# Where two units' weight forms are made, and when modulation 5 is computed, in a one-core mixer and feed-forward block

## The chip, the cores and the metric

The kernel runs on one core of a Trainium2 chip. The metric is the device time of one execution, in microseconds (us). Five engines take part, each with its own stream of instructions that it works through in order: TensorE (matrix products; in the profile PE, its weight loads PEld), VectorE (DVE), ScalarE (ACT), GpSimd (POOL) and SyncE (SP, which here only issues transfers). GpSimd can issue transfers too.

## The reference

One layer of a transformer-like block on 1024 tokens of width 1024, all in float32:

```python
px = modulate(x, mx[0], mx[1]) @ w_in            # 1024 x 4864
mix_x = token_mixers(px, ...)                     # a two-way gated scan with 4 heads, a short convolution, a spatial gate
x_new = layer_norm(x * ALPHA + mx[2] * (mix_x @ w_out), ln1_g, ln1_b)
ffn_x = conv_ffn(modulate(x_new, mx[3], mx[4]), ffn_up, conv_w, conv_b, ffn_down)
x_new = layer_norm(x_new * ALPHA + mx[5] * ffn_x, ln2_g, ln2_b)
```

The six modulations `mx` are rows of `silu(c) @ ada_w + ada_b`. In `conv_ffn` the product with `ffn_up` (1024 x 5632) gives two halves a and g of 2816 columns each; a goes through a 3x3 convolution over a 16 x 64 grid and a GELU, is multiplied by g, and then by `ffn_down`.

## The kernel before

**Split products.** A float32 matrix is written as a high part (rounded to TensorE's fp32r format) and a low part (the remainder), and a product is three TensorE products: high x high, high x low, low x high. ScalarE makes the high part with a copy, VectorE or GpSimd the low part with a subtraction (`split`).

**Stages.** `startup` normalises and transposes x and makes the first projections. `mixers` runs the projections of w_in, head by head, between the steps of the scan: `z_head(h)` is three projections (`proj`), each of 48 TensorE products; `scan_levels` and `scan_states` are mostly VectorE and ScalarE work. `out_proj` multiplies by w_out, one tile t of 128 tokens after another, eight in all: 48 products a tile, then the sum with x (`ly`), the layer norm (`ln_rows`), and, for two tiles at a time, `modulate2`, which normalises again (`norm2`) and transposes for the feed-forward part. The mixers' outputs are split for tile t + 2 (tiles `mh`, `ml`) while tile t is worked on. `ffn_up` makes 22 units of 128 columns of a and g, and `ffn_down` the last product.

**Forms.** In `ffn_up` a unit's two 2 x 2 blocks of products are made by a Strassen-like scheme with seven products instead of eight. For them seven forms of the unit's weights are needed: four of the weights' quarters (a11, a12, a21, a22) or sums of them (S1 = a21 + a22, S2 = S1 - a11, a11 - a21, a12 - S2), each split into a high and a low part: 128 x 2 x 512 numbers, 512 KB. Product k of a unit is 12 TensorE products of 512 columns, in the order k = 1, 2, 6, 5, 7, 3, 4. From unit 3 on, ScalarE and GpSimd make the forms on the fly (`prepare`, five products ahead). Unit 0 is multiplied plainly. The forms of units 1 and 2 are made beforehand and parked in device memory: `park` gives a list of steps (load, sums, one step for each form), and `out_proj` runs one of them after the fourth and the eighth weight tile of each half. All of a step's arithmetic is on GpSimd, which also issues the stores. Forms 1 and 2 of unit 1 are not parked: `load_form` makes them in tile t = 6 of `out_proj`, ScalarE the high part, GpSimd the low part.

**Order.** Up to the end of `out_proj` a scheduler orders each engine's instructions from a model of their cost and from priorities (program order, with loads and their splits far ahead). In `ffn_up` everything stays in program order (`pinned`). Work that may be done at any time lies in the list `self.aside`, and `step(n)` takes n pieces from it; `proj` calls `step(2)`. In `mixers` it is empty until the modulations 2 to 4 are put into it, ahead of head 3.

**Tiles.** Tag S has 13 buffers of 4 KB a partition, which the mixers, w_out and `ffn_up` share; tag W has six, for weights and forms; tag R four, for raw loads. PSUM has two pairs of banks (`psA`) and four single banks (`psB`).

**Modulation 5.** Its eight columns (40 to 47) are made in `ffn_up`, two in each of the units 5, 7, 9 and 11, after product 6: `ada_col` is one VectorE reduction of 128 x 1024 (in the profile CUSTOM_DVE_ANT_0 on `ada`), a read of the accumulator and a small sum. Unit f's VectorE work in order: the sum a after product 5, two products h of the unit before, the sum r after product 7, the other half of a after product 3, and then the convolution, eight operations on a pair of banks. ScalarE copies r after product 5, and `centre` writes the convolution's middle tap into the pair of banks that product 3 goes on with.

Nearly all instructions are recorded under line 57, a helper; they are told apart by tiles.

Of the kernel before, what the change touches and what calls it, by code (L numbers as in the profile page):

```python
# [7 lines left out]
F32 = mybir.dt.float32  # L8
F32R = mybir.dt.float32r
# [7 lines left out]
P = 128  # L17
# [50 lines left out]
class Builder:  # L68
# [433 lines left out]
    def mixers(self, head, vt, gc):  # L502
        hd = [head] + [dict() for _ in range(H - 1)]
        O = [None] * H
        self.consts2()
        self.scan_prep(hd[0], 0)
        cx = self.ctx_prep()
        sc = [self.short_conv(0, gc)]
        self.scan_levels(hd[0])
        self.ctx_states(*cx)  # L510
        self.scan_prep(hd[1], 1, self.z_head(1))
        O[0] = self.scan_states(hd[0], 0, vt)
        self.scan_levels(hd[1])
        self.scan_prep(hd[2], 2, self.z_head(2))
        O[1] = self.scan_states(hd[1], 1, vt)
        self.scan_levels(hd[2])
        self.sc = self.S(nm="silc")
        self.nc.sync.dma_start(self.sc, self.silc[0:1].broadcast_to([P, D]))
        self.aside += self.more_mods(16, 24)
        vt = self.v_pair(1)  # L520
        self.scan_prep(hd[3], 3, self.z_head(3))
        O[2] = self.scan_states(hd[2], 2, vt)
        self.scan_levels(hd[3])
        self.aside += self.more_mods(24, 40)
        self.gate_head(O[0], 0)
        sc.append(self.short_conv(1))
        O[3] = self.scan_states(hd[3], 3, vt)
        self.aside = self.wout_load(range(5)) + self.aside
        for h in range(1, H - 1):
            self.gate_head(O[h], h)  # L530
        sg = self.spatial_gate()
        self.gate_head(O[H - 1], H - 1)
        self.step(99)
        self.mix = O + sc + sg
# [385 lines left out]
    def out_proj(self, op):  # L920
        nc, a = self.nc, self.a
        for part in self.wout_load(range(5, KT), op):
            part()
        lng, lnb = (self.row(n, op.tile([P, D], F32, name=n)) for n in ("ln1_g", "ln1_b"))
        order, wh, wl = self.order, self.wh, self.wl
        mhl = {}
        self.parked = {}
        parks = self.park(op, 1, (6, 5, 7, 3, 4)) + self.park(op, 2, (1, 2, 6, 5, 7, 3, 4))

        def split(t):  # L930
            mh, ml = self.S((KT, P), F32R, nm="mh"), self.S((KT, P), F32R, nm="ml")
            for kt in order:
                self.split(self.mix[kt][:, t * P:(t + 1) * P], mh[:, kt, :], ml[:, kt, :])
            mhl[t] = mh, ml

        split(0)
        split(1)
        ys = {}
        for t in range(NT):
            mh, ml = mhl.pop(t)  # L940
            banks = [self.bank("A") for _ in range(2)]
            for c in range(2):
                s = slice(c * 512, (c + 1) * 512)
                for kt in order:
                    self.mm3(banks[c], mh[:, kt, :], ml[:, kt, :], wh[kt][:, s], wl[kt][:, s], kt == order[0], kt == order[-1])
                    if c == 1:
                        self.step(1)
                    if parks and kt in (order[3], order[7]):
                        parks.pop(0)()
            y = ys[t] = self.S(nm="ly") if t % 3 == 2 or t == 7 else self.At(nm="ly")  # L950
            nc.sync.dma_start(y, a["x"][t * P:(t + 1) * P])
            if t + 2 < NT:
                split(t + 2)
            if t in (2, 4):
                self.aside += self.modulate2([ys[t - 2], ys[t - 1]], t - 2)
            if t == 6:
                self.first = [self.load_form(1, 0), self.load_form(1, 1)] + [self.load_unit(a["wup"][f], (KT, P)) for f in (0, FT)]
                self.raws = {}
            for c in range(2):
                s = slice(c * 512, (c + 1) * 512)  # L960
                nc.vector.scalar_tensor_tensor(out=y[:, s], in0=y[:, s], scalar=ALPHA, in1=banks[c], op0=ALU.mult, op1=ALU.add)
            if t == 7:
                self.norm2([ys[j] for j in (4, 5, 6)])
            self.ln_rows(y, lng, lnb)
            nc.sync.dma_start(self.xnew[t], y)
        return [ys[t] for t in range(4, 8)]
# [36 lines left out]

    FORM = {1: "11", 2: "21", 3: "22", 4: "T4", 5: "T1", 6: "T2", 7: "T3"}

    def load_form(self, u, i):

        w = self.Wt((2, 512), nm="wf")
        with self.tc.high_priority(self.AHEAD):
            raw = self.Rt((4, P))  # L1010
            self.nc.sync.dma_start(raw, self.a["wup"][u][:, 4 * i:4 * i + 4])
            self.split(raw.rearrange("p k f -> p (k f)"), w[:, 0], w[:, 1], self.nc.gpsimd)
        return w

    def load_raws(self, u):
        ra, rg = self.S((2, 512), nm="raw"), self.S((2, 512), nm="raw")
        for r, f in ((ra, u), (rg, FT + u)):
            self.nc.sync.dma_start(r.rearrange("p j (k f) -> p (j k) f", f=P), self.a["wup"][f])
        self.raws[u] = dict(a=ra, g=rg)

    def park(self, op, u, ks):

        nc, pool = self.nc, self.nc.gpsimd
        r = {}

        def raws():
            for i, f in enumerate((u, FT + u)):
                r[i] = op.tile([P, 2, 512], F32, tag="raw", bufs=2, name=self.name("raw"))
                nc.sync.dma_start(r[i].rearrange("p j (k f) -> p (j k) f", f=P), self.a["wup"][f])

        def parts():
            return r[0][:, 0], r[0][:, 1], r[1][:, 0], r[1][:, 1]

        def sums():
            a11, a12, a21, a22 = parts()
            s = self.Wt((2, 512), F32, nm="ws")
            r["S1"], r["S2"] = s[:, 0], s[:, 1]
            pool.tensor_tensor(out=r["S1"], in0=a21, in1=a22, op=ALU.add)
            pool.tensor_tensor(out=r["S2"], in0=r["S1"], in1=a11, op=ALU.subtract)

        def sums2():
            a11, a12, a21, a22 = parts()
            pool.tensor_tensor(out=a12, in0=a12, in1=r["S2"], op=ALU.subtract)
            pool.tensor_tensor(out=a21, in0=a11, in1=a21, op=ALU.subtract)

        def one(k):
            a11, a12, a21, a22 = parts()
            src = {1: a11, 2: a12, 3: a12, 4: a22, 5: r.get("S1"), 6: r.get("S2"), 7: a21}[k]
            w = self.Wt((2, 512), nm="wp")
            pool.tensor_copy(w[:, 0], src)  # L1050
            pool.tensor_tensor(out=w[:, 1], in0=src, in1=w[:, 0].bitcast(F32), op=ALU.subtract)
            d = self.parked[u, k] = self.dp.tile([P, 2, 512], F32, name=self.name("wd"))
            nc.gpsimd.dma_start(d, w.bitcast(F32))
        one_ = lambda k: lambda: one(k)
        early = [k for k in ks if k < 3]
        return [raws, sums] + [one_(k) for k in early] + [sums2] + [one_(k) for k in ks if k not in early]

    def prepare(self, n):

# [6 lines left out]
        while self.prepared < min(n + 1, len(self.plan)):  # L1066
            u, k = self.plan[self.prepared]
            self.prepared += 1
            if (u, k) in self.parked:
                self.forms[u, k] = self.Wt((2, 512), nm="wf")  # L1070
                nc.sync.dma_start(self.forms[u, k].bitcast(F32), self.parked[u, k])
                continue
            r = self.raws[u]
            a11, a12, a21, a22 = r["a"][:, 0], r["a"][:, 1], r["g"][:, 0], r["g"][:, 1]
# [38 lines left out]
    def ffn_up(self, ys):  # L1113
# [45 lines left out]
        def sums(j):  # L1159
            b12, b22, b11 = v[j][:, 0], v[j][:, 1], xa[j]  # L1160
            return [lambda: tt(out=b22, in0=b22, in1=b12, op=ALU.subtract),
                    lambda: tt(out=b12, in0=b12, in1=b11, op=ALU.subtract),
                    lambda: tt(out=b11, in0=b22, in1=b11, op=ALU.add)]
# [109 lines left out]
        for f in range(3, FT):  # L1273
            if f + 2 < FT:
                self.load_raws(f + 2)
            if f in (5, 7, 9, 11):
                silc = self.S(nm="silc5")
                nc.sync.dma_start(silc, self.silc[0:1].broadcast_to([P, D]))
                ada = [self.S(nm="ada") for _ in range(2)]
                for i in range(2):  # L1280
                    nc.sync.dma_start(ada[i], self.a["ada"][35 + f + i])
            if f == last:
                ahead = self.down_first()
            while self.at < len(self.plan) and self.plan[self.at][0] == f:
                k = self.plan[self.at][1]
                step()
                if f == last:
                    ahead(k)
                if k == 6 and f in (5, 7, 9, 11):
                    for i in range(2):  # L1290
                        j = 35 + f + i
                        self.ada_col(j, silc, self.mods[:, j:j + 1], [ada[i]])
            if f == 12:
                self.gate5 = self.gate_line(5)
        self.prev.gelu()
# [276 lines left out]
```

## Time and profile before

| | |
|---|---|
| median of three runs | 1369.55 us (1369.33 to 1370.62) |
| the profiled execution | 1371.46 us, its span 1369.7 us |
| TensorE busy | 1284.1 us, 94% of the span |
| VectorE busy | 977.1 us, 71% |
| ScalarE busy | 528.3 us, 39% |
| GpSimd busy | 334.1 us, 24% |
| mean granted TensorE clock | 0.983 |
| moved by the transfer engines | 177.09 MB, mean 129 GB/s |

The span runs from the first to the last instruction of the program. By the time at which their tiles appear, the mixers run up to about 540 us, w_out from 540.9 to 661 us, `ffn_up` from there to about 1110 us, and `ffn_down` after that. The page's slices are 34.2 us long each, and a digit is the busy share in tenths. A row of the timeline gives start, length, engine, line, operation, the tiles written and read, and in brackets how long the engine stood idle before it and what released it. In a row of the windows each engine has its busy time and its count of instructions, and the last three numbers are the granted clock, the mean busy share of the 16 transfer engines and GB/s.

### The profile page before, as it was taken

Reading aid. Unit: us, or ns where it says so; the run is one execution under the profiler, and the core shown is the slowest. Engines: PE = TensorE matmul, PEld = TensorE weight load, DVE = VectorE, ACT = ScalarE, POOL = GpSimd, SP = SyncE. Lnnn points to the kernel's source line nnn. Section 1 sums busy time; section 2 is a strip of 40 time slices with the busy share of each in tenths; the row PEclk is TensorE's granted clock in tenths of the full one; section 3 lists DMA queues with packets and bytes.
Section 4 is the critical chain, followed back from the end, with each engine's and each line's share of the span. In section 5 each row is a group of like instructions: output and inputs, shape, how many; then the busy total and the mean of one; then the engine's idle time right before and its main releaser. Section 6 shows DMA issues by size and latency. Waiting matters only on the chain. (4 is left out here: it accounts for less than half of the span.)

```text
span 1369.7 us, 17583 instructions
## 1 busy us (share of the span) xinstructions
PE 1284.1 (94%) x6480; PEld 1074.6 (78%) x6480; DVE 977.1 (71%) x1712; ACT 528.3 (39%) x966; POOL 334.1 (24%) x279
## 2 busy tenths in 40 slices
PE   4999999999999999949998999999999999999997
PEld 3878988898888797737876877778888887887885
DVE  7868963778669587788797767776776664349447
ACT  4745443432432331135463434344444434323420
POOL 0000000000000000560027766677777740000000
PEclk9999999999999999969999999999999999999999
DMA  9662320023121353545452332332122218447532
GB/s 331 241 223 86 108 92 33 31 80 106 47 92 62 105 161 108 197 168 177 150 190 87 138 132 71 122 138 74 65 93 93 77 69 296 167 152 247 178 97 86
DMA packets 70406, 177.09 MB, mean 129 GB/s; under 512 B 8224, under 2 KB 10928, under 8 KB 70320
## 3 DMA queue, kind: packets, MB, share of 16 engines
q1 hardware_dynamic: 68304, 168.63, 36.2%
q0 software_dynamic: 2016, 7.34, 1.3%
q8 instruction: 51, 0.84, 0.2%
q14 instruction: 35, 0.29, 0.1%
HBM read 147.61 MB, written 28.33 MB: 128 GB/s over the span
## 5 line engine op out<-in xcount | busy, mean ns | idle before, releaser
L57 DVE SCALAR_TENSOR_TENSOR psA<-a,par,psA 128x945 f32<-128x945 f32 (+2 forms) x176 | 215.9, 1227 | 21.6 <-ACT psA L57 16.2
L57 PE MATMUL psA<-x,wf 128*128 128x512 f32 x708 | 175.7, 398 | 15.2 <-ACT psA L57 11.8
L57 PE MATMUL psB<-xk,wf 128*128 128x512 f32 x672 | 176.8, 390 | 1.0 <-ACT s L57 1.0
L57 PEld LDWEIGHTS psA<-x,wf 128*128 128x128 f32 x708 | 135.5, 192 | 46.6 <-ACT psA L57 14.3
L57 PEld LDWEIGHTS psB<-xk,wf 128*128 128x128 f32 x672 | 126.2, 188 | 27.9 <-ACT s L57 1.4
L57 POOL TENSOR_TENSOR wf<-raw,wf 128x512 fp32r<-128x512 f32 x95 | 124.5, 1322 | 62.8 <-ACT wf L57 62.7
L57 PE MATMUL psA<-xh,wh 128*128 128x512 f32 x320 | 127.4, 398 | 2.1 <-ACT wh L57 1.2
L57 PE MATMUL psA<-xh,wl 128*128 128x512 f32 x320 | 126.6, 396 | 0.1
L57 PE MATMUL psA<-xl,wh 128*128 128x512 f32 x320 | 126.6, 396 | 0.0
L57 POOL TENSOR_TENSOR ws<-raw 128x512 f32<-128x512 f32 x2 | 2.6, 1282 | 460.3 <-DMA raw<-in_wup 460.3
L57 DVE TENSOR_TENSOR dwl<-r,dwh 128x512 fp32r<-128x512 f32 x74 | 48.4, 688 | 81.1 <-ACT dwh L57 81.0
L57 PE MATMUL psB<-x,wf 128*128 128x512 f32 x384 | 104.7, 389 | 0.0
L57 PE MATMUL psB<-dwh,dh 128*128 128x512 f32 x296 | 98.5, 394 | 2.9 <-ACT dh L57 2.9
L57 PE MATMUL psA<-dwh,dh 128*128 128x512 f32 x296 | 97.3, 390 | 0.7 <-DVE fy L57 0.7
L57 PEld LDWEIGHTS psB<-x,wf 128*128 128x128 f32 x384 | 72.1, 188 | 15.4 <-issue 0.2
L57 ACT CAST dwh<-r 128x512 fp32r<-128x512 f32 x74 | 43.0, 619 | 102.8 <-PE psA L57 67.0
L57 ACT CAST wh<-r 128x512 fp32r<-128x512 f32 x76 | 44.6, 618 | 92.1 <-PE psA L57 64.5
L57 DVE TENSOR_TENSOR a<-psA,s 128x512 f32<-128x512 f32 x39 | 26.9, 691 | 72.1 <-PE psA L57 72.1
L57 DVE TENSOR_TENSOR wl<-r,wh 128x512 fp32r<-128x512 f32 x76 | 49.9, 685 | 36.1 <-ACT wh L57 22.8
L57 ACT CAST wf<-raw 128x512 fp32r<-128x512 f32 x95 | 58.5, 616 | 42.3 <-PE psA L57 27.4
L57 PEld LDWEIGHTS psA<-xh,wh 128*128 128x128 f32 x320 | 60.5, 189 | 14.2 <-ACT wh L57 1.6
L57 PEld LDWEIGHTS psA<-xh,wl 128*128 128x128 f32 x320 | 60.6, 189 | 12.5 <-DVE wl L57 0.5
(328 smaller groups left out, 2813.8 us busy)
## 6 DMA issues: line engine op xcount, KB each, us to landing
raw<-in_wup SPq DMA_DIRECT2D x42, 512.0 KB, 4.8
r<-in_w_down SPq DMA_DIRECT2D x82, 256.0 KB, 3.3
ada<-in_ada SPq DMA_DIRECT2D x32, 512.0 KB, 3.8
r<-in_win SPq DMA_DIRECT2D x56, 256.0 KB, 2.7
hr<-hd SPq DMA_DIRECT2D x41, 256.0 KB, 4.2
hd<-h SPq DMA_DIRECT2D x20, 512.0 KB, 3.0
adat<-in_ada SPq DMA_DIRECT2D x16, 512.0 KB, 6.9
wd<-wp POOLq DMA_DIRECT2D x12, 512.0 KB, 3.8
```

Source lines behind the costliest of these rows:

```text
L57: ins = f(*args, **kw)
```

## The change

1. `park` no longer works form by form on GpSimd. A unit is now done in four chunks, the k-th 128 columns of each quarter in one tile of 128 x 8 x 128: four quarters from device memory and the four sums S1, S2, a11 - a21 and a12 - S2, which VectorE makes (`sums(c)`, four operations of 128 x 128). `store(c)` then makes the high part of all eight with one ScalarE copy of 128 x 1024 and the low part with one VectorE subtraction; GpSimd only issues the two stores.
2. Unit 1's eight steps go into `self.aside` of `mixers`, behind `ctx_states`, so that the `step(2)` calls of the next projections take them; its tiles have tag S. Unit 2's eight steps run in `out_proj`, one after the products of each tile t.
3. A form is read back with two transfers, one for the high and one for the low part, in pieces of 128 numbers (`parked_form`). Forms 1 and 2 of unit 1 are read back in the same way at t = 6; `load_form` goes.
4. Modulation 5 is made one column in each of the units 4 to 11, after product 7 instead of 6, with the bias given to the reduction as its start value, so that the small sum goes.

```diff
         self.ctx_states(*cx)
+        self.parked = {}
+        self.aside += self.park(1, lambda dt: self.S((8, P), dt, nm="pk"))
         self.scan_prep(hd[1], 1, self.z_head(1))
...
-        parks = self.park(op, 1, (6, 5, 7, 3, 4)) + self.park(op, 2, (1, 2, 6, 5, 7, 3, 4))
+        parks = self.park(2, lambda dt: op.tile([P, 8, P], dt, tag="pk", bufs=2, name=self.name("pk")))
...
-                    if parks and kt in (order[3], order[7]):
-                        parks.pop(0)()
+            parks.pop(0)()
...
-                self.first = [self.load_form(1, 0), self.load_form(1, 1)] + [...]
+                self.first = [self.parked_form(1, 1), self.parked_form(1, 2)] + [...]
...
+        def sums(c):
+            r = t[c] = new(F32)
+            for i, f in enumerate((u, FT + u)):
+                nc.sync.dma_start(r[:, 2 * i:2 * i + 2], self.a["wup"][f].rearrange("p (j k) f -> p j k f", j=2)[:, :, c])
+            a11, a12, a21, a22, s1, s2, s3, s4 = (r[:, i] for i in range(8))
+            tt(out=s1, in0=a21, in1=a22, op=ALU.add)
+            tt(out=s3, in0=a11, in1=a21, op=ALU.subtract)
+            tt(out=s2, in0=s1, in1=a11, op=ALU.subtract)
+            tt(out=s4, in0=a12, in1=s2, op=ALU.subtract)
+        def store(c):
+            r, h = t[c], new(F32R)
+            nc.scalar.copy(h, r)
+            nc.gpsimd.dma_start(d[:, 0, c], h.bitcast(F32))
+            tt(out=r.bitcast(F32R), in0=r, in1=h.bitcast(F32), op=ALU.subtract)
+            nc.gpsimd.dma_start(d[:, 1, c], r)
+        return [lambda c=c, f=f: f(c) for c in range(4) for f in (sums, store)]
+
+    def parked_form(self, u, k):
+        w = self.Wt((2, 512), nm="wf")
+        i = {1: 0, 2: 1, 3: 7, 4: 3, 5: 4, 6: 5, 7: 6}[k]
+        for j in range(2):
+            self.nc.sync.dma_start(w[:, j].bitcast(F32).rearrange("p (c f) -> p c f", c=4), self.parked[u][:, j, :, i])
+        return w
...
-            if f in (5, 7, 9, 11):
-                silc = self.S(nm="silc5")
+            if 4 <= f < 12:
+                silc, ada = self.S(nm="silc5"), self.S(nm="ada")
                 nc.sync.dma_start(silc, self.silc[0:1].broadcast_to([P, D]))
-                ada = [self.S(nm="ada") for _ in range(2)]
-                for i in range(2):
-                    nc.sync.dma_start(ada[i], self.a["ada"][35 + f + i])
+                nc.sync.dma_start(ada, self.a["ada"][36 + f])
...
-                if k == 6 and f in (5, 7, 9, 11):
-                    for i in range(2):
-                        j = 35 + f + i
-                        self.ada_col(j, silc, self.mods[:, j:j + 1], [ada[i]])
+                if k == 7 and 4 <= f < 12:
+                    j = 36 + f
+                    nc.vector.tensor_tensor_reduce(out=ada, in0=ada, in1=silc, scale=1.0, scalar=self.par[:, C_ADAB + j:C_ADAB + j + 1],
+                                                   op0=ALU.mult, op1=ALU.add, accum_out=self.mods[:, j:j + 1])
```

More of the change, by code (lines that the diff above doesn't have):

```diff
@@ L926, in out_proj @@
         mhl = {}
-        self.parked = {}
-        parks = self.park(op, 1, (6, 5, 7, 3, 4)) + self.park(op, 2, (1, 2, 6, 5, 7, 3, 4))
+        parks = self.park(2, lambda dt: op.tile([P, 8, P], dt, tag="pk", bufs=2, name=self.name("pk")))
         def split(t):
@@ L956, in out_proj @@
             if t == 6:
-                self.first = [self.load_form(1, 0), self.load_form(1, 1)] + [self.load_unit(a["wup"][f], (KT, P)) for f in (0, FT)]
+                self.first = [self.parked_form(1, 1), self.parked_form(1, 2)] + [self.load_unit(a["wup"][f], (KT, P)) for f in (0, FT)]
                 self.raws = {}
@@ L1004 @@
     FORM = {1: "11", 2: "21", 3: "22", 4: "T4", 5: "T1", 6: "T2", 7: "T3"}
[L1006 to L1013, printed above, removed]
     def load_raws(self, u):
@@ L1019, in load_raws @@
         self.raws[u] = dict(a=ra, g=rg)
[L1021 to L1026, printed above, removed]
-            for i, f in enumerate((u, FT + u)):
[L1028 to L1056, printed above, removed]
@@ new lines, in park @@
+    def park(self, u, new):
+        nc, tt = self.nc, self.nc.vector.tensor_tensor
+        d = self.parked[u] = self.dp.tile([P, 2, 4, 8, P], F32, name=self.name("wd"))
+        t = {}
+        def sums(c):
+            r = t[c] = new(F32)
+            for i, f in enumerate((u, FT + u)):
+                nc.sync.dma_start(r[:, 2 * i:2 * i + 2], self.a["wup"][f].rearrange("p (j k) f -> p j k f", j=2)[:, :, c])
[11 more added lines that the diff above has]
+        return [lambda c=c, f=f: f(c) for c in range(4) for f in (sums, store)]
@@ L1068, in prepare @@
             self.prepared += 1
-            if (u, k) in self.parked:
-                self.forms[u, k] = self.Wt((2, 512), nm="wf")
-                nc.sync.dma_start(self.forms[u, k].bitcast(F32), self.parked[u, k])
+            if u in self.parked:
+                self.forms[u, k] = self.parked_form(u, k)
                 continue
```

## The prediction

> **What bounds the kernel now.** I read the page's slices first, then TensorE's waits, then the windows around each dip, and last the instructions there in order of time.
>
> ```profile
> span 1369.7 us, 17583 instructions
> PE   4999999999999999949998999999999999999997
> PEclk9999999999999999969999999999999999999999
> ```
>
> TensorE is busy nearly everywhere, so only its holes can be won. Slice 17 (from 582 us) is half empty, and the granted clock falls to 0.6 there. That is w_out, where GpSimd makes the parked forms. In these windows the pairs are PE, PEld, DVE, ACT and POOL busy time, then the granted clock:
>
> ```profile
> 540.90:585.90 45.00, 41.49 (x171) 31.61 (x171) 37.59 (x81) 13.63 (x50) 18.74 (x21) 1.00 0.47 172
> 585.90:600.30 14.40, 0.00 (x0) 0.00 (x0) 14.40 (x16) 1.25 (x2) 14.36 (x18) 0.58 0.26 106
> 600.30:612.10 11.80, 8.79 (x25) 6.47 (x26) 8.66 (x18) 5.23 (x12) 5.97 (x7) 0.50 0.70 272
> 612.10:648.00 35.90, 35.90 (x166) 28.50 (x165) 28.38 (x87) 18.05 (x56) 0.29 (x1) 1.00 0.47 159
> ```
>
> TensorE stands still for 14.4 us while VectorE and GpSimd are both full; then it works at half clock; after GpSimd falls silent it is full. The timeline says why (start, length, instruction, in brackets the idle time before it and its releaser):
>
> ```profile
> 568.07 0.73 PE L57 MATMUL psA<-wok,mh 128*128 128x512 f32 x2 [1.51 <-DVE ly L57]
> 600.35 0.48 PE L57 MATMUL psB<-ident,ly 128*128 128x128 f32 x1 [14.52 <-ACT ly L57]
> 607.20 0.90 PE L57 MATMUL psB<-ident,ly 128*128 128x128 f32 x3 [2.96 <-ACT ly L57]
> ...
> 599.05 1.24 ACT L57 ACTIVATE ly<-ly,nmt,rst 128x1024 f32<-128x1024 f32 x1 [15.10 <-DVE nmt L57]
> ...
> 549.19 0.28 DVE L57 TENSOR_TENSOR ml<-O,mh 128x128 fp32r<-128x128 f32 x1
> 589.64 5.47 DVE L57 TENSOR_TENSOR ml<-sgo,mh 128x128 fp32r<-128x128 f32 x2
> 595.03 3.14 DVE L57 TENSOR_TENSOR ml<-O,mh 128x128 fp32r<-128x128 f32 x1
> ...
> 595.55 2.47 POOL L57 TENSOR_TENSOR wp<-ws,wp 128x512 fp32r<-128x512 f32 x2
> ```
>
> A subtraction ml of 0.28 us takes 3.14 us and ends (598.17) just after two of GpSimd's (598.02). VectorE, in order, then reaches nmt late, ScalarE's ly waits 15.10 us for it, and the first transpose of modulate2 waits 14.52 us for ly. So VectorE's two-input operations wait for GpSimd's.
>
> The second loss is in ffn_up. The chain of waits shows the units' boundaries (12 products of 512 take 2.72 us, a unit of seven takes 19.04):
>
> ```profile
> 773.94 5.44 PE psB L57 x24
> ...
> 797.04 5.46 PE psB L57 x24
> ...
> 816.11 5.44 PE psB L57 x24
> ...
> 920.28 4.76 PE psB L57 x21
> ```
>
> Unit 5, with two ada columns, takes 23.10 us; unit 6, without, 19.07. From 773.94 to 920.28 there are seven units, 5 to 11: 146.34 us, 13.1 more than 7 x 19.04, all in the four units that carry columns.
>
> **The change part by part.** *GpSimd's forms leave w_out.* This takes away the hole (14.4), in the next 11.8 us everything but what 15 products of 512 (0.23 each, 2.72/12) and 10 transposes (about 0.13) cost at full clock, 4.8, so 7.0, and the 1.51 at 568: 22.9 us. It takes VectorE's waits too:
>
> ```profile
> L57 DVE TENSOR_TENSOR ml<-O,mh 128x128 fp32r<-128x128 f32 x32 | 17.5, 563 | 8.7 <-PE psA L57 5.4 <-PE psB L57 2.9 <-ACT mh L57 0.2
> L57 DVE TENSOR_TENSOR ml<-sgo,mh 128x128 fp32r<-128x128 f32 x16 | 10.0, 661 | 0.0
> L57 DVE TENSOR_TENSOR ml<-sco,mh 128x128 fp32r<-128x128 f32 x16 | 6.9, 467 | 0.0
> ...
> L57 DVE TENSOR_TENSOR kq<-kq,F 128x1024 f32<-128x1024 f32 x56 | 67.4, 1214 | 0.2
> ```
>
> The 64 ml subtractions took 34.4 us where 64 x 0.28 is 17.9: 16.5 us of waiting.
>
> *Unit 2's forms come to VectorE and ScalarE there.* A chunk costs VectorE four small operations (0.28) and one of 1024 (1.21, the kq row): 2.3 us, four chunks 9.3; ScalarE one copy of 1024, about 1.1 (twice the 0.61 of a 512 cast, below), 4.6 in all, where it is two thirds idle. VectorE's four windows above hold 89.0 us; less 16.5, plus 9.3, that is 81.8, against 107.1 - 22.9 = 84.2 us that TensorE would then need. VectorE is thus close behind TensorE. The copy and the differences queue ahead of split(t+2) and the ly sums, on which the transposes wait. What stays of stalls is between 0 (81.8 fits) and the whole 9.3; I take 3, since ml is not the only operation that got stretched, so that the true load is lower, but the load is uneven. Later, load_form's two casts and two GpSimd operations also go.
>
> *Unit 1's forms go among the mixers*: 9.3 us of VectorE, 4.6 of ScalarE, eight steps, six in z_head(1), two in z_head(2).
>
> ```profile
> 200.00:220.00 20.00, 20.00 (x90) 16.56 (x89) 3.98 (x6) 8.45 (x14) 0.00 (x0) 1.00 0.16 53
> ```
>
> In z_head(1) VectorE is busy 4 of 20 us and GpSimd not at all, so I count 0. The cover is TensorE's own full row; were it gone, the price is 9.3. New waits: each chunk's two loads stand on SP among the w_in loads and need one of 13 S tiles; behind a stuck load wait the next w_in pieces, behind a stuck difference on VectorE the wl splits. Those run about one projection ahead. Bounds -1 to +5 (half of the 9.3; a rearranged order can also gain).
>
> *Stores and loads.* GpSimd issues 16 stores instead of 12, at a time when it does nothing else. SP issues 16 chunk loads of 128 KB instead of four raws of 512 KB (half of them now among the mixers), and 28 form loads instead of 14 (12 wf, load_form's two), in 512-byte pieces instead of 4 KB; at 0.3 to 0.5 us an issue this fills no queue. At the start of ffn_up a form is eaten every 2.72 us:
>
> ```profile
> 698.00:702.00 4.00, 4.00 (x18) 2.96 (x17) 4.00 (x7) 3.90 (x8) 0.10 (x1) 1.00 0.98 388
> ...
> 636.00:637.00 1.00, 1.00 (x8) 0.86 (x8) 0.40 (x2) 1.00 (x4) 0.00 (x0) 1.00 1.02 401
> ```
>
> The forms now move at 388 GB/s with the transfer engines full; a microsecond of xr stores (1 KB pieces) shows 401. At 300 GB/s a form of 512 KB would take 1.7 us, under 2.72. No row has 512-byte pieces in bulk; I take 0, bounds 0 to +8. The Trainium skill ("DMA: Bandwidth & Descriptors", Specifications) puts the smallest transfer for line rate at 512 B; by it these loads would cost nothing more, and no row here shows it.
>
> *Modulation 5, one column a unit, after product 7.* SP loads silc eight times instead of four, a unit ahead of its use; two S tiles a unit are held instead of three every second one. The reduction, without the small sum behind it, moves from between the convolution and the sum a to behind the sum r. A unit without columns, and the old reductions of unit 7:
>
> ```profile
> 798.69 10.06 DVE L57 SCALAR_TENSOR_TENSOR psA<-a,par,psA 128x945 f32<-128x945 f32 x8 [0.85 <-ACT psA L57]
> 813.50 0.69 DVE L57 TENSOR_TENSOR r<-psB,r 128x512 f32<-128x512 f32 x1 [0.83 <-ACT wf L57]
> 816.22 0.69 DVE L57 TENSOR_TENSOR a<-psA,s 128x512 f32<-128x512 f32 x1 [2.03 <-PE psA L57]
> 827.73 2.27 DVE L57 CUSTOM_DVE_ANT_0 ada<-ada,silc 128x1024 f32<-128x1024 f32 x1
> 831.10 1.21 DVE L57 CUSTOM_DVE_ANT_0 ada<-ada,silc 128x1024 f32<-128x1024 f32 x1
> ...
> 809.76 0.61 ACT L57 CAST wf<-raw 128x512 fp32r<-128x512 f32 x1
> 811.50 0.59 ACT L57 COPY r<-psA 128x512 f32<-128x512 f32 x1 [1.13 <-DVE a L57]
> 812.12 0.78 ACT L57 ACTIVATE psA<-a,par 128x512 f32<-128x512 f32 x1
> ...
> 813.23 2.88 PE L57 MATMUL psA<-x,wf 128*128 128x512 f32 x12
> ...
> 813.52 1.29 POOL L57 TENSOR_TENSOR wf<-s,wf 128x512 fp32r<-128x512 f32 x1 [1.78 <-ACT wf L57]
> ...
> 817.26 1.31 POOL L57 TENSOR_TENSOR raw<-raw,s 128x512 f32<-128x512 f32 x1
> ```
>
> Between r's end (814.19) and the next a (816.22) VectorE waits 2.03 us: room for 1.21. If the reduction ends later by D, a and the convolution shift by D; ScalarE has 1.1 us of slack before r's copy and 0.3 before product 3, so TensorE pays only what D has over 1.4. GpSimd works from 813.52 to 818.57 (four operations, first and last shown), so the reduction may be held up. One operation long (it starts at 814.77) it ends at 816.0 and costs nothing; two long, at 817.2, D = 1.0, still nothing; three long, at 818.5, D = 2.3, it costs 0.9 a unit. I take 0 and the full 13.1; bounds 0 to 15. The Trainium skill ("SBUF — State Buffer", Who interferes with whom) says that a VectorE instruction with two SBUF inputs contends with a GpSimd one that reads SBUF, and that whichever issues first blocks the other until it is done; by that the reduction waits for one operation and the sum is mine. The 3.14 us row outlasted two, so the row leaves the rival below open.
>
> **The sum.** The profiled execution took 1371.46 us (span 1369.7). 1371.5 - 22.9 + 3 - 13.1 = 1338.5. It stands 1.9 above the median of the runs, 1369.55, so 1336.6, said as 1337.
>
> **The rivals.** A: VectorE becomes the bound of w_out and all 9.3 us come on the path instead of 3: 1343. For it speaks 81.8 of 84.2; against it that TensorE stayed full in 612 to 648 with VectorE at 28 of 36. B: the reduction waits for three GpSimd operations: 8 x 0.9, and a slow restart as in unit 5 (4.06 us lost for a wait of 2.2) about doubles it, 7 to 15 us: 1344 to 1352. For it: 813.52 to 818.57 has no gap. Against: the old ones lost 1.06 us at most. C: the mixers pay up to 5 for unit 1's steps: 1337 to 1342. D, the other side: the form loads of 512-byte pieces fall behind. Ten forms are eaten in a row after 700 us. To eat all 33 us each must come 3.3 late, one per 6.0 us, that is 87 GB/s; below this the kernel is slower than before (at 60 GB/s, 8.7 us a form, by 27: 1397). Against it stand 388 and 401 GB/s. E: the change does not do what it says, that is, the hole is VectorE's own load and stays: then only the 13.1 come, 1356. Against: the 0.28 against 3.14 us.
>
> **How the numbers follow.** My forecast (1330 to 1340) 0.55; A 0.14; B 0.13; C 0.08; D and all that turns the sign 0.04; E 0.06. The range 1327 to 1351 holds the forecast, A, C and most of B, some 0.87 at most by these chances. Two runs of this kernel tell apart about 0.2%, 2.7 us. Faster: 0.95; same 0.01; slower 0.04.
>
> **What would show it.** After: no slice under 8 between 540 and 680 us, granted clock 1.00 there, no GpSimd operation in w_out but stores, ml at 0.28 us; seven units 5 to 11 in 133 to 134 us, with ada reductions of 1.2 to 3.5 us behind r; the same full TensorE row in z_head(1) and (2); no wait of TensorE for a transfer of wf. It is wrong if a transpose in w_out still waits for ly over 5 us, if product 3 waits for ScalarE's psA in units 4 to 11, or if TensorE has new holes between 190 and 300 us.

## The result, and the profile after

| | before | after |
|---|---|---|
| median of the four runs | 1369.53 us | 1335.52 us (without the fourth 1335.19) |
| the profiled execution | 1371.46 us, its span 1369.7 | 1334.04 us, its span 1332.1 |
| TensorE busy | 1284.1 us, 94% | 1275.0 us, 96% |
| VectorE busy | 977.1 us | 963.9 us |
| ScalarE busy | 528.3 us | 536.7 us |
| GpSimd busy | 334.1 us | 307.0 us |

The ratio is 0.9746, 95% interval 0.9727 to 0.9766; the forecast was 1337, from 1327 to 1351. Three of the four times of after lie between 1334.04 and 1335.85 us; the fourth, 3283.34 us, is explained by nothing on record, and the ratio leaves it out. In a later series the same kernel took 1335.78 us (1334.16 to 1337.52).

The slices of after come first (33.3 us each). Slice 17 is full now, and the granted clock has no dip there:

```profile
span 1332.1 us, 17666 instructions
PE   4999999999999999999988999999999999999997
PEclk9999999999999999999998999999999999999999
```

The new dip, slices 20 and 21, is the beginning of ffn_up from 666 us; its losses were there before, 23 us later. A ledger by stage, from TensorE's first products of each stage in both traces, in us:

| stage | before | after | difference |
|---|---|---|---|
| start to the first product of w_out | 540.90 | 539.93 | -1.0 |
| w_out, to the first product of ffn_up | 120.08 | 97.07 | -23.0 |
| ffn_up to the end of unit 4 | 112.96 | 114.54 | +1.6 |
| units 5 to 11 | 146.34 | 133.51 | -12.8 |
| unit 12 to the first steady piece of w_down | 218.15 | 216.20 | -1.95 |
| the rest | 231.27 | 230.85 | -0.4 |

The two stages that were to gain bring 35.8 of the 37.6 us between the two spans. First w_out. Its windows after (PE, PEld, DVE, ACT, POOL busy time with counts, granted clock, share of the transfer engines, GB/s), and beside them z_head(1), which was shown before:

```profile
539.93:584.93 45.00, 44.26 (x187) 34.20 (x187) 40.16 (x122) 18.56 (x56) 2.13 (x4) 1.00 0.38 131
584.93:637.00 52.07, 50.45 (x230) 40.26 (x231) 44.26 (x127) 25.95 (x73) 2.13 (x4) 1.00 0.58 197
...
200.00:220.00 20.00, 20.00 (x90) 16.57 (x89) 6.68 (x12) 9.38 (x15) 1.83 (x4) 1.00 0.47 167
```

TensorE works 94.7 of 97.07 us at full clock. VectorE is busy 84.4 us in the stage. The same stage of before, as one window, shows what it was busy with:

```profile
540.90:660.98 120.08, 99.16 (x417) 77.01 (x417) 101.90 (x228) 41.33 (x125) 41.61 (x46) 0.90 0.46 165
```

VectorE had 20 instructions fewer there and was busy 101.9 us. The 20 are unit 2's (tiles pk). Without them the stage of after is busy 77.4 us: they last 9.0 us by themselves, but neighbouring records overlap by up to 0.1 us, so they add only 7.0. The instructions that both kernels have thus took 101.9 us before and 77.4 after, about 24 us of mere waiting. The groups name it: 17.9 us are ml (34.4 before; 8.5 + 4.0 + 4.0 = 16.5 after, 0.28 us each on average), 4.9 two operations on one column (nwt), 1.4 an operation of the layer norm (`ly`). The groups of after, with the new operations on pk of both units, at the prices taken for them:

```profile
L57 DVE TENSOR_TENSOR pk<-pk,pk 128x1024 fp32r<-128x1024 f32 x8 | 9.7, 1215 | 4.7 <-ACT pk L57 4.6
L57 DVE TENSOR_TENSOR ml<-O,mh 128x128 fp32r<-128x128 f32 x32 | 8.5, 283 | 0.2 <-PE psA L57 0.2
L57 ACT CAST pk<-pk 128x1024 fp32r<-128x1024 f32 x8 | 8.4, 1049 | 10.9 <-DVE pk L57 9.1 <-issue 1.9
L57 DVE TENSOR_TENSOR pk<-pk 128x128 f32<-128x128 f32 x32 | 8.2, 280 | 4.6 <-DMA pk<-in_wup 4.4
L57 DVE TENSOR_TENSOR ml<-sgo,mh 128x128 fp32r<-128x128 f32 x16 | 4.0, 284 | 0.0
L57 DVE TENSOR_TENSOR ml<-sco,mh 128x128 fp32r<-128x128 f32 x16 | 4.0, 284 | 0.0
```

Even an operation on one column had been held up (it has two inputs, vet and rst). The larger of the two groups on nwt, in the stage of before, and then in after:

```profile
L57 DVE TENSOR_TENSOR nwt<-vet,rst 128x1 f32<-128x1 f32 x12 | 5.3, 442 | 0.0
```

```profile
L57 DVE TENSOR_TENSOR nwt<-vet,rst 128x1 f32<-128x1 f32 x12 | 1.8, 149 | 0.0
```

TensorE's waits of after, from 540 to 1100 us (in total, times, longest): ly has 1.7 us left of 17.5, and the waits for psA 3.1 of 11.8.

```profile
PE psA L57 <- ACT h L57: 3.4, 1, 3.4
PE psA L57 <- ACT psA L57: 3.1, 2, 1.8
PE psB L57 <- ACT dh L57: 2.6, 1, 2.6
PE psB L57 <- ACT ly L57: 1.7, 2, 1.4
```

Then the units. In the chain of waits of after units 5 to 11, each of which has a column now, take 133.51 us, 19.07 each, the time of unit 6 without columns in before (unit 8, whose reduction lasted 2.19 us, took 19.27, the others 19.04):

```profile
751.54 5.44 PE psB L57 x24
770.58 5.44 PE psB L57 x24
789.62 5.44 PE psB L57 x24
...
866.01 5.44 PE psB L57 x24
885.05 5.44 PE psB L57 x24
```

The timeline of one unit shows how the reduction meets GpSimd (start, length):

```profile
787.00 0.69 DVE L57 TENSOR_TENSOR r<-psB,r 128x512 f32<-128x512 f32 x1 [0.82 <-ACT wf L57]
787.60 1.81 DVE L57 CUSTOM_DVE_ANT_0 ada<-ada,silc,par 128x1024 f32<-128x1024 f32 x1
789.73 0.69 DVE L57 TENSOR_TENSOR a<-psA,s 128x512 f32<-128x512 f32 x1 [0.31 <-PE psA L57]
...
787.04 1.29 POOL L57 TENSOR_TENSOR wf<-s,wf 128x512 fp32r<-128x512 f32 x1 [1.75 <-ACT wf L57]
788.30 2.27 POOL L57 TENSOR_TENSOR raw<-raw,raw 128x512 f32<-128x512 f32 x1
```

The reduction, 1.21 us long by itself, starts at 787.60 and ends 0.6 us later than it would alone: it waits for the one GpSimd operation under way (to 788.33). Then GpSimd's next operation lasts 2.27 instead of 1.29: now GpSimd waits. The sum a still finds 0.31 us of idle time ahead of it, so TensorE pays nothing.

### The profile page after: what moved, and what is told of

Read it like the earlier page. It is cut to its first block, busy times and chain, and to the rows that moved or that the text cites. A ratio compares the mean times of both kernels' runs of the same rounds, so it can differ in the third digit from the quotient of the medians.

```text
span 1332.1 us, 17666 instructions
## 1 busy us (share of the span) xinstructions
PE 1275.0 (96%) x6480; PEld 1069.2 (80%) x6480; DVE 963.9 (72%) x1744; ACT 536.7 (40%) x972; POOL 307.0 (23%) x249
## 5 line engine op out<-in xcount | busy, mean ns | idle before, releaser
L57 POOL DMA_DIRECT2D wd<-pk x16 | 8.7, 543 | 498.9 <-ACT pk L57 461.3
L57 PEld LDWEIGHTS psA<-xl,wh 128*128 128x128 f32 x320 | 60.2, 188 | 11.8 <-issue 0.2
```

The costliest lines, as they stand in the source:

```text
L57: ins = f(*args, **kw)
```

## The experiments

There are ten runs, in three series, each beside the kernel before on the same chip.

**The parts by themselves.** `mod5_only` is the kernel before with the new modulation 5; `forms_only` is the changed kernel with the old one.

> The kernel before with the new modulation 5 alone (one column in each of units 4 to 11, after product 7); the forms are made by GpSimd in w_out as before. Theory (the two gains are separate stretches of TensorE's path and add up): units 5 to 11 take 133.3 to 133.6 us instead of 146.3, the hole in w_out stays as it was, time 1356 to 1357. Rival (the change's halves need each other, or the gain in the units is given back at the start of w_down): 1360 to 1369.

> The changed kernel with the old modulation 5 (two columns in units 5, 7, 9 and 11, after product 6). Theory: w_out stays about 97 us long (540 to 637), units 5 to 11 take 146 us again, time 1347 to 1350, that is 13 more than the changed kernel; with the run of modulation 5 alone the two gains add up to the whole of 34 within 2. Rival (part of the w_out gain was only that units meet another phase of the clock): 1340 to 1346 or over 1351.

Measured: modulation 5 alone 1356.43 us against 1368.40, ratio 0.9918 (0.9899 to 0.9936); forms alone 1344.61, ratio 0.9829 (0.9811 to 0.9848). By the ratios the parts gain 0.82% and 1.71%, together 2.53%, and the whole change gained 2.54%: the parts add up within the uncertainty (0.002 is 2.7 us). TensorE's waits show that with modulation 5 alone the hole of w_out is all there, and with the forms alone the units' waits:

```profile
PE psB L57 <- ACT ly L57: 17.1, 2, 15.8
```

```profile
PE psA L57 <- ACT psA L57: 11.7, 6, 2.2
```

The kernel with the forms alone was 2.4 us faster than its expected range, and its time lies in the range given to the rival, that the gain of w_out was in part another phase of the clock. The trace doesn't bear the rival out: w_out takes 97.8 us there (542.3 to 640.1), as in the changed kernel. Its units 5 to 11 took 144.7 us instead of 146.3 for a reason that comes up again below: one unit fewer at half the granted clock. The rest of the miss lies within the spread of its runs (1343.47 to 1348.18 us).

**Is it GpSimd's reading that holds VectorE up?** Two kernels are the changed one with work put back on GpSimd that nobody waits for, in the tiles 0 to 5 of w_out:

```diff
+            if t < 6:
+                zz = self.Wt((2, 512), F32, nm="zz")
+                nc.scalar.copy(zz[:, 0], banks[1])
+                nc.gpsimd.tensor_copy(zz[:, 1], zz[:, 0])
+                for _ in range(6):            # pool_two_in
+                    nc.gpsimd.tensor_tensor(out=zz[:, 1], in0=zz[:, 0], in1=zz[:, 1], op=ALU.subtract)
+                for _ in range(14):           # pool_memset, instead of the six
+                    nc.gpsimd.memset(zz[:, 1], 0.0)
```

> The changed kernel, plus work that nobody waits for: in each of the w_out tiles 0 to 5, tied to the end of that tile's products by a ScalarE copy, GpSimd does one copy and six subtractions of 128 x 512 from SBUF into a scratch tile, 36 subtractions, some 46 us in all. Theory (VectorE's operations with two SBUF inputs wait for GpSimd's operations that read SBUF): ml and the pk operations are stretched again to 1 to 3 us, VectorE falls behind, TensorE waits in w_out, time 1350 to 1366. Rival (the hole came from what the old forms did to order, buffers or transfers, not from GpSimd running beside VectorE): 1335 to 1338 and ml stays at 0.28 us.

> The same as the run with six subtractions a tile, but with 14 GpSimd memsets of 128 x 512 in their place, which write SBUF and read nothing. Theory (only GpSimd operations that read SBUF hold VectorE up): ml stays near 0.28 us but for the one copy a tile, time 1335 to 1339. Rival (any GpSimd access to SBUF holds VectorE up): stretched ml as in the other run, in proportion to the memsets' time.

Measured: with the subtractions 1365.84 us, ratio 0.9981 (0.9969 to 0.9992); with the memsets 1339.54, ratio 0.9782 (0.9757 to 0.9807). GpSimd is busy for much the same time in both. The groups, first with the subtractions, then with the memsets:

```profile
L57 POOL TENSOR_TENSOR zz<-zz 128x512 f32<-128x512 f32 x36 | 50.8, 1412 | 2.7
L57 DVE TENSOR_TENSOR ml<-O,mh 128x128 fp32r<-128x128 f32 x32 | 18.2, 583 | 1.9 <-ACT mh L57 1.9
```

```profile
L57 POOL MEMSET zz<- 128x512 f32 x84 | 43.9, 527 | 4.2
L57 DVE TENSOR_TENSOR ml<-O,mh 128x128 fp32r<-128x128 f32 x32 | 8.5, 282 | 2.0 <-PE psA L57 1.2 <-ACT mh L57 0.7
```

36 subtractions that nothing waits for cost, with the copies that feed them, 30 us against the changed kernel, and TensorE waits for ly again (`psB <- ly` 18.9 us, longest 9.8); ml is 0.58 us on average, less than the 1 to 3 us expected. 84 memsets leave ml at 0.28 us. The memset kernel also has six GpSimd copies, which read one input, and VectorE is held up beside three of them. Here is one, and below it two subtractions ml beside it, which last 0.90 us where two such elsewhere in this trace take 0.48:

```profile
560.96 0.69 POOL L57 COPY zz<-zz 128x512 f32<-128x512 f32 x1 [1.23 <-ACT zz L57]
561.09 0.90 DVE L57 TENSOR_TENSOR ml<-sgo,mh 128x128 fp32r<-128x128 f32 x2
```

So the hole is made by GpSimd's reading, not by its being busy. The Trainium skill ("SBUF — State Buffer", Who interferes with whom) says that a VectorE instruction with two SBUF inputs contends with a GpSimd one that reads SBUF; both kernels agree, 0.583 us against 0.282. The memset kernel stands about 4 us above the changed one, half a microsecond above what was expected, with runs from 1334.10 to 1341.71 us. In its profiled execution unit 3 of ffn_up ends 5.2 us later than in the changed kernel: 2.1 us of this are lost before w_out, where nothing was edited, and 3.1 in w_out, with one stretch of 3.4 us at a granted clock of 0.50 (from 614.6 us) and a wait for ly that is 1.2 us longer. What the six ScalarE copies and the six GpSimd copies have in that wasn't tried.

**One column or two, product 6 or 7.** Modulation 5 had changed in place and in number. `one_after6` changes back the place, `two_after7` the number:

```diff
-                if k == 7 and 4 <= f < 12:
+                if k == 6 and 4 <= f < 12:                  # one_after6
+                if k == 7 and f in (5, 7, 9, 11):           # two_after7
+                    for i in range(2):                      # ... columns 35 + f + i
```

> The changed kernel with modulation 5 one column a unit in units 4 to 11, but after product 6, between the convolution and the sum a. Theory (what cost the old form its 13 us was two reductions in a row, 4.7 us, in a place with 2.0 us of room; one of 1.2 to 1.9 us nearly fits anywhere): a is at most 0.5 us late, product 3 waits 0.1 to 0.4 us a unit, units 5 to 11 in 134 to 136 us, time 1335 to 1339. Rival (the place after product 7 is what matters): TensorE waits over 1 us in each of eight units with slow restarts, units 5 to 11 over 141 us, time 1343 to 1350.

> The changed kernel with two columns in units 5, 7, 9 and 11, as before, but after product 7 and with the bias as start value. Theory (room of 2.0 us before the next sum a, and 1.4 us of slack behind it): the two take 3.0 to 3.7 us, a is 1.1 to 1.8 us late, TensorE waits 0 to 0.4 us in four units, units 5 to 11 in 133.3 to 136 us, time 1335 to 1340. Rival (the slack behind a is less than I read, or two reductions each lose a whole GpSimd operation): over 1 us in each of the four units, with slow restarts 4 to 12 us in all, 1340 to 1348.

Measured: one a unit after product 6, 1332.20 us, ratio 0.9724 (0.9701 to 0.9747); two after product 7, 1337.06, ratio 0.9754 (0.9732 to 0.9777). VectorE's timeline, first with one column after product 6, then with two after product 7:

```profile
780.85 2.26 DVE L57 CUSTOM_DVE_ANT_0 ada<-ada,silc,par 128x1024 f32<-128x1024 f32 x1
783.04 0.68 DVE L57 TENSOR_TENSOR a<-psA,s 128x512 f32<-128x512 f32 x1
785.63 0.69 DVE L57 TENSOR_TENSOR r<-psB,r 128x512 f32<-128x512 f32 x1 [0.72 <-ACT psA L57]
```

```profile
766.46 0.69 DVE L57 TENSOR_TENSOR r<-psB,r 128x512 f32<-128x512 f32 x1 [0.83 <-ACT wf L57]
767.07 1.80 DVE L57 CUSTOM_DVE_ANT_0 ada<-ada,silc,par 128x1024 f32<-128x1024 f32 x1
768.80 2.31 DVE L57 CUSTOM_DVE_ANT_0 ada<-ada,silc,par 128x1024 f32<-128x1024 f32 x1
771.04 0.68 DVE L57 TENSOR_TENSOR a<-psA,s 128x512 f32<-128x512 f32 x1
```

After product 6 the reduction waits a whole GpSimd operation (2.26), but VectorE has caught up before r (0.72 us idle): seven units take 133.4 us, slightly less than the 134 to 136 expected. With two in a row after product 7, a starts 4.58 us after r (771.04 - 766.46), where it was 2.72 without a reduction (813.50 to 816.22 in before): 1.86 us late. Less the 1.4 us of slack that leaves 0.46, and a pair of units takes 38.6 instead of 38.08 us. So with one column a unit the place is free. With two it isn't: after product 7 a unit loses 0.5 us, where the old pair after product 6 lost 2.5 to 4.1. The old pair was also longer, 4.70 us from its start at 785.57 to the next a at 790.27 in before, and 1.13 of that was a small sum on one column (the other small sum took 0.16), which the change does away with. How much the place saves and how much the dropped sum wasn't tried apart. The first time of `one_after6`, 3 us below the changed kernel's and below its own expected range, was put to the test, both in one series:

> The changed kernel once more, beside the variant with the reduction after product 6, so that the two stand on one chip. Expected 1334 to 1337 us, ratio about 0.975. If the reduction's place matters, the variant will stand apart from it by more than 2.7 us; if only the count of columns in a unit matters, the two agree.

> One column a unit after product 6. By the theory that only the count per unit matters: the same as the changed kernel within 2.7 us, although each reduction is longer (2.26 us in its first run, against 1.81). By the rival that this place is better (first run 1332.2 us): 3 us or more below the changed kernel in the same call.

Measured: 1335.78 us, ratio 0.9762 (0.9741 to 0.9783), and 1334.71, ratio 0.9749 (0.9725 to 0.9772). The two can't be told apart. The 3 us were not a gain.

**Where the two units go.** The change puts unit 1 among the mixers and unit 2 into w_out. `both_wout` has both in w_out, two steps a tile; `both_mixers` both among the mixers:

```diff
-        self.aside += self.park(1, ...)                      # both_wout: in out_proj,
+        parks = self.park(1, new) + self.park(2, new)        # two steps after each tile
...
+        self.aside += self.park(1, new) + self.park(2, new)  # both_mixers: none in out_proj
```

> The changed kernel with unit 1's eight steps in w_out too, two steps a tile (unit 1 in tiles 0 to 3, unit 2 in 4 to 7), none among the mixers. Theory (VectorE is close behind TensorE there: 81.8 of 84.2 us by my estimate; 9.3 more make it the bound): w_out 4 to 10 us longer than 97, time 1339 to 1346. Rival (the estimate of VectorE's load was too high, there is room for both): 1334 to 1338.

> The changed kernel with unit 2's eight steps among the mixers too, behind unit 1's, none in w_out. Theory (VectorE has idle time in the projections, and w_out has only 1.7 us of waits left to give): 1332 to 1337, TensorE's waits among the mixers (15 to 536 us) no more than 2 us longer. Rival (16 steps push into scan_levels, where VectorE is the bound, or run out of the 13 S tiles): TensorE waits 3 us or more longer among the mixers, 1338 to 1346.

Measured: both in w_out 1343.29 us, ratio 0.9802 (0.9777 to 0.9827); both among the mixers 1339.53, ratio 0.9776 (0.9749 to 0.9803). Unit 3 of ffn_up ends at 732.48 us in the changed kernel, at 741.79 with both in w_out and at 737.56 with both among the mixers. Of the 9.3 us of the first, -0.6 come before w_out, 2.7 in it (99.7 us; 4 to 10 more had been expected) and 7.2 behind it, at the first products of ffn_up. That they equal the VectorE work of one unit to the tenth is chance: they are made of waits and of TensorE's half clock (0.50 for 6.8 us from 651.2). The timeline of ScalarE there, and the product that waits:

```profile
646.77 1.05 ACT L57 CAST pk<-pk 128x1024 fp32r<-128x1024 f32 x1 [5.56 <-DVE pk L57]
...
652.15 1.24 ACT L57 ACTIVATE ly<-ly,nmt,rst 128x1024 f32<-128x1024 f32 x1 [0.60 <-DVE nmt L57]
...
653.48 0.56 ACT L57 COPY s<-psB 128x512 f32<-128x512 f32 x1
...
654.09 4.82 PE L57 MATMUL psB<-x,wf 128*128 128x512 f32 x12 [6.63 <-ACT s L57]
```

The copy s stands on ScalarE behind the cast of a late pk and the layer norm's ly, both waiting for VectorE, which is behind with its sums; TensorE then waits 6.63 us for s and resumes slowly (4.82 us for 12 products, 2.72 at full clock).

Among the mixers the theory, that the second unit is hidden too, fell and the rival held. Unit 2's steps come past the heads' projections into the scan, whose operations wait behind them; the waits for the scan's tiles A and kq show it:

```profile
PE psB L57 <- ACT A L57: 4.3, 4, 3.6
PE psA L57 <- ACT kq L57: 1.8, 1, 1.8
```

From 15 to 536 us TensorE waits 22.5 us there, against 18.1 in the changed kernel. Behind the longest wait for A, which ends at 267.99, it also works at a granted clock of 0.50 for 10.2 us (from 268.7). So w_out begins 8.5 us later (548.4 us), of which w_out, without steps of its own, gives 1.8 back (95.2 us). No variant beat the changed kernel by more than the measurement can tell.

## Why the prediction was right, point by point

- *The hole of w_out, 22.9 us, of which 3 stay.* The 22.9 held, the 3 did not: w_out is 23.0 us shorter, so nothing stayed on balance. The mis-sized term is VectorE's load. In the first 84.2 us of the stage VectorE was busy 71.9 us, where 81.8 was worked out. The prediction took off only ml's waits, 16.5 us (17.9 measured), where about 24 went, for operations on one column and of the layer norm had been held up too; the prediction named that possibility and its direction. And it added unit 2's work at 9.3, which adds only 7.0 to the busy time.
- *Rival A, VectorE as the bound of w_out*, gave 1343 for all 9.3 us on the path. It did not come for unit 2. With unit 1 there as well the time was 1343.29, but that the numbers agree is chance: only 2.7 us were lost in w_out, the rest behind it.
- *Unit 1 among the mixers at nothing.* Held: TensorE is full in the window of z_head(1) between 200 and 220 us, and the stage up to w_out is 1.0 us shorter, inside -1 to +5. The 1.0 need not be a gain of the change: before has a stretch of 3.4 us at a granted clock of 0.50 there (from 103.5 us), after has none. `both_mixers` shows that the cover ends there: the second unit made the mixers 8.5 us longer.
- *The form loads at nothing.* Held, on a narrower cover than the row of before suggested. 14 of them are issued from 669.94 to 680.8 us, and the transfer engines are full at 303 GB/s, where the old forms had 388 (the second window, 314, has 4 KB pieces of raw in it too):

```profile
675.00:680.00 5.00, 4.84 (x20) 3.31 (x18) 4.37 (x8) 4.90 (x10) 0.00 (x0) 1.00 1.17 303
680.00:685.00 5.00, 3.90 (x17) 3.24 (x18) 4.89 (x7) 2.28 (x5) 0.00 (x0) 1.00 1.20 314
```

  The issues' row of after gives the median time to landing, 5.1 us for 256 KB; in before it was 3.9 for 512 KB.

```profile
wf<-wd SPq DMA_DIRECT2D x28, 256.0 KB, 5.1
```

  No product waits for a transfer of wf, and rival D (87 GB/s) is far off. The Trainium skill ("DMA: Bandwidth & Descriptors", Specifications) puts the smallest transfer for line rate at 512 B; here 512-byte pieces moved at about 0.8 of the rate of 4 KB pieces (303 against 388), so the measurement does not bear that out, though the sum did not need it. The prediction's row of 401 GB/s says nothing of 1 KB pieces: all 98 data packets recorded in that microsecond are of 4 KB, and xr's begin in the next one.
- *Modulation 5, 13.1 us.* Measured 12.8 for units 5 to 11. The reduction waits for one GpSimd operation, as taken, and ends at 1.81 us; rival B's three did not occur in any of the eight (1.81 to 2.19). The slack of 1.4 us was borne out by the two columns after product 7: 1.86 us late, 0.5 us lost. That the gain was 13 and not 10 is in part luck of the profiled execution of before. Its four units with columns have the same wait of 2.18 us ahead of product 3, but the twelve products behind it differ:

```profile
792.44 4.60 PE psA L57 x12
834.61 3.01 PE psA L57 x12
875.16 4.49 PE psA L57 x12
917.23 3.06 PE psA L57 x12
```

  In the first and the third the granted clock is 0.50 for 3.4 us (from 793.0 and 874.9), in the others 1.00. The kernel with the forms alone has the same four waits and one such stretch. So the prediction's slow restart, which about doubles a loss, does not come with every wait, and some 3 us of the 13.1 hang on it.
- *The sum.* 1338.5 for the profiled execution, which took 1334.04: 4.5 us less. 3.1 come from w_out, -0.3 from the units; the other 1.7 are small and outside the change's steps: -1.0 before w_out, +1.6 at the start of ffn_up, -1.95 and -0.4 behind unit 12. The +1.6 and 1.6 of the -1.95 go with stretches of 3.4 us at a granted clock of 0.50: up to unit 4 of ffn_up before has one (from 738.4) and after two (714.5 and 728.2), and at the beginning of w_down before has one (1134.4), where 12 products took 4.60 us, and after none (3.02). The changed kernel's later profile has such a stretch there again (1096.6), so that part is luck.

## What to carry to other kernels

When an instruction takes many times its usual length, look which other engine ends at the same moment: here the time belonged to GpSimd's instruction, and the cure was to take its reading away, not to make the slow one shorter. Freed in this way, a vector engine has more room than its busy time showed, but that room has an edge: here one unit of 9.3 us fitted under the products, and with a second one in the same place the kernel took some 8 us longer. Work that can go anywhere is best spread in pieces that fit the room and the slack of one repetition (2.0 and 1.4 us a unit here); then the exact place hardly mattered.

## What the runs showed of the hardware that was not expected

- Held-up time spreads to operations that hardly read anything: `nwt`, one column of 128 numbers, took 0.44 us on average beside GpSimd and 0.15 without.
- The hold-up goes both ways: GpSimd's subtraction takes 1.29 us, and 2.27 when VectorE's reduction came first; 36 of them beside w_out averaged 1.41.
- GpSimd's memsets, 84 in 43.9 us, did not hold VectorE's largest group up (ml from O, 0.282 us; 0.283 without them); single GpSimd copies did.
- In pieces of 512 bytes the full transfer engines moved 303 GB/s, in pieces of 4 KB 388.
- Equal waits of TensorE (2.18 us) are followed by 3.4 us at a granted clock of 0.50 in some cases and by none in others, in one and the same execution.
